# Lower halves of four w_up blocks made on GpSimd in a hybrid decoder layer

## Chip, cores and metric

The kernel runs on one core of one Trainium2 chip. The metric is the device time of one execution in microseconds; of several executions the median is given. The engines are called TensorE (PE in the rows; its weight loads are PEld), VectorE (DVE), ScalarE (ACT), GpSimd (POOL) and SyncE (SP, which issues most DMAs here).

## What is computed

One decoder layer on a sequence of 512 tokens with 1024 features, all in float32. An attention group and a recurrent group share one input projection; their outputs are joined by w_out, normalised and added to x; then comes a gated feed-forward part with a causal convolution of width 3 and another norm. Cut to what matters here:

```python
    mix = jnp.concatenate([attn, lru], axis=-1) @ w_out[l].astype(h.dtype)
    x = x + rms_norm(mix, g_post_mix[l])
    h = rms_norm(x, g_pre_ffn[l])
    up = causal_dwconv(h @ w_up[l].astype(h.dtype), w_conv_ffn[l], b_conv_ffn[l])
    c_u, c_g = jnp.split(up, 2, axis=-1)
    ffn = (jax.nn.gelu(c_g, approximate=True) * c_u) @ w_down[l].astype(h.dtype)
    x = x + rms_norm(ffn, g_post_ffn[l])
```

w_up is 1024 x 5632: 22 blocks of 128 columns for c_u and 22 for c_g.

## The kernel before

Every large product is made of three TensorE products on halves: a float32 operand is split into an upper half h (a rounded copy in the type that TensorE reads, made by ScalarE) and a lower half l = x - h, made by VectorE unless `split` is given another engine (L83 to L85). `mm3` (L77 to L81) then issues h times h (L79), one h with the other's l (L80) and the reverse (L81). `split_w` (L92) does it for a piece of a weight, 128 x 1024 here, from a tile `raw` that a DMA filled; there are four buffers for each half and two for `raw`.

The place in question is the passage from w_out to w_up. `wide` (L738) makes the product with w_out in two column halves; in the second one, for the token tiles t = 0 to 3 of 128 rows each, 24 products go into `py`t (L79 to L81), then `weighted` (L713) squares the result on ScalarE, multiplies it by the gain on VectorE (L725) and makes the reciprocal root `rpost` (L135 to L141: small 128x1 operations), and `mixed` (L768) adds it to the residual `xres` (two operations at L733), squares that on ScalarE (`sqn`, L150), makes `rpre` in the same way, scales (`hn`, L154), transposes on TensorE (`ptr`, L160, eight in two banks), and splits the result into h2Th (ScalarE, L84) and h2Tl (VectorE, L85, reading the bank). So tile after tile goes through a chain over VectorE, ScalarE and TensorE.

Meanwhile the first four blocks of w_up have been split into tiles of their own (`fw00` to `fw11`, `load_first_up`, L787). The loop at L833 takes four blocks a turn, `i2` = 0 to 10: two of c_u and two of c_g. For i2 = 0 the products run in two column halves of 256 tokens (L842 to L844), so that the first half needs only the tiles t = 0 and 1; that makes 96 products of 256 columns for each half. For i2 = 1 and on, four `split_w` calls (L839) make the blocks, and the products have 512 columns. For i2 = 1 these splits have no other work ahead of them than the chain of the norm.

Up to L182 the order of instructions on each engine is the written one. Behind it a scheduler orders them by its own estimate, engine by engine, as buffers and data come free; each engine then works its list strictly in order. In the list of VectorE the four subtractions of i2 = 1 (tiles wl_2498, wl_2503, wl_2508 and wl_2513) stand between the steps of the chain.

Of the kernel before, what the change touches and what calls it, by code (L numbers as in the profile page):

```python
# [18 lines left out]
P = 128  # L19
# [8 lines left out]
KD = D // P  # L28
# [24 lines left out]
def hybrid_layer(  # L53
# [6 lines left out]
    nc = tc.nc  # L60
# [9 lines left out]
    def bank(name, tag):  # L70
        return ps.tile([P, 512], F32, tag=tag, name=name, bufs=BANKS[tag])
# [11 lines left out]
    def split(h, l, src, sub=None):  # L83
        nc.scalar.copy(h, src)  # L84
        (sub or nc.vector).tensor_sub(l, src, f32(h))  # L85

    def load_raw(src, k, n):
        t = wp.tile([P, k, n], F32, tag="raw", name="raw", bufs=2)
        nc.sync.dma_start(t, src.rearrange("(k p) n -> p k n", p=P))
        return t  # L90

    def split_w(src, k, n, sub=None):  # L92
        h = wp.tile([P, k, n], F32R, tag="wh", name="wh")
        l = wp.tile([P, k, n], F32R, tag="wl", name="wl")
        split(h, l, src, sub)
        return h, l
# [688 lines left out]
    first_up = [[], []]  # L785
# [26 lines left out]
    def up(w, pt, c0, c1):  # L812
        for k in range(KD):
            mm3(pt[:, c0:c1], at(w, slice(None), k), at(h2T, slice(None), k, slice(c0, c1)),
                k == 0, k == KD - 1)
# [9 lines left out]
    def glu(i, pu, pg):  # L825
        yu = conv(pu, i, "yu")
        yg = conv(pg, NF + i, "yg")
        nc.scalar.activation(yg, yg, AF.Gelu_apprx_tanh)  # L828
        nc.vector.tensor_mul(yu, yu, yg)  # L829
        split(*act_at(i, slice(None)), yu)  # L830

    up_tags = itertools.cycle(("mm", "sc", "mm", "sc", "mm", "av"))
    for i2 in range(NF // 2):  # L833
        if i2:
            raws = [load_raw(w_up[:, o + 256 * i2:o + 256 * (i2 + 1)], KD, 256) for o in (0, DFF)]
        blocks = [[], []]
        for b in range(2):
            for j in range(2):
                w = split_w(raws[j][:, :, b * P:(b + 1) * P], KD, P) if i2 else first_up[b][j]  # L839
                blocks[b].append((w, bank("pup", next(up_tags))))  # L840
        if i2 == 0:
            for c0, c1 in ((0, S // 2), (S // 2, S)):  # L842
                for w, pt in blocks[0] + blocks[1]:
                    up(w, pt, c0, c1)  # L844
        for b in range(2):
            if i2:
                for w, pt in blocks[b]:
                    up(w, pt, 0, S)
            glu(2 * i2 + b, blocks[b][0][1], blocks[b][1][1])
        if i2 == 0:  # L850
            f_stack.close()
            actp2 = ctx.enter_context(tc.tile_pool(name="actp2", bufs=1, side="right"))
            acts.append([actp2.tile([P, NF - NF1, S], F32R, name=f"act{i}") for i in "hl"])
# [45 lines left out]
```

## Time and profile before

| | us |
|---|---|
| median of 3 runs | 585.64 (584.77 to 586.01) |
| the profiled execution | 584.45 |
| its span, first to last instruction | 582.3 |
| TensorE busy | 571.0 (98%) |
| VectorE busy | 360.1 (62%) |
| ScalarE busy | 279.3 (48%) |
| GpSimd busy | 15.9 (3%), the last of it at 96 us |

A row of a timeline gives the start, the duration, the engine, the line, the operation and what it writes and reads; in brackets, how long the engine was idle ahead of it and what ended that. Successive instructions of one engine overlap a little in their rows, so the step from start to start is shorter than a duration.

### The profile page before, as it was taken

The numbers are of one execution on the slowest core, as the hardware profiler recorded it, in microseconds if no ns is written. First come the engines' busy times: TensorE is split into PE (matmuls) and PEld (weight loads), VectorE is DVE, ScalarE is ACT, GpSimd is POOL, SyncE is SP. The second block draws the span as 40 slices with busy tenths as digits, with TensorE's granted clock in tenths as the row PEclk, the third lists the DMA queues.
The fourth block names the chain that finished last, engine by engine and source line by source line (L and its number), as shares of the span: only waits on it lengthen the run. The fifth ranks groups of instructions, "written<-read, shape, count | busy, mean of one in ns | idle before, by whom it ended". The sixth has DMA issues, their size and how long they took to land.

```text
span 582.3 us, 7051 instructions
## 1 busy us (share of the span) xinstructions
PE 571.0 (98%) x2734; PEld 472.9 (81%) x2734; DVE 360.1 (62%) x649; ACT 279.3 (48%) x457; POOL 15.9 (3%) x37
## 2 busy tenths in 40 slices
PE   8999999999999999999999999999999999999995
PEld 4988887887788789888888888888888888888884
DVE  5797777889896895656656656656656521241225
ACT  6568846868776663543443444444444321132121
POOL 2150000000000000000000000000000000000000
PEclk9999999999999999999999999999999999999998
DMA  9533627333202614013412412412413222332103
GB/s 275 152 110 122 205 72 200 94 106 108 74 1 72 217 41 142 1 49 96 145 55 90 144 60 86 146 64 81 144 66 136 88 72 90 100 136 73 37 0 144
DMA packets 53450, 59.62 MB, mean 102 GB/s; under 512 B 2481, under 2 KB 42625, under 8 KB 53418
## 3 DMA queue, kind: packets, MB, share of 16 engines
q1 hardware_dynamic: 53319, 59.11, 31.9%
q8 instruction: 21, 0.34, 0.2%
q14 instruction: 12, 0.09, 0.1%
q10 hardware_dynamic: 98, 0.07, 0.0%
HBM read 57.06 MB, written 3.69 MB: 104 GB/s over the span
## 4 chain that ended last, share of the span: by engine, by line
PE 90%; DVE 4%; ACT 3%; DMA 2%; issue 0%; DVEq 0%; SPq 0%; ACTq 0%
PE pup L80 14%; PE pup L81 14%; PE pup L79 14%; PE py L80 8%; PE py L79 8%; PE py L81 8%; PE px L309 3%; PE pq L79 2%; PE pq L80 2%; PE pq L81 2%; PE pav L663 2%; PE ptp L653 1%; PE pgr L81 1%; PE pgr L80 1%; PE pv L81 1%; PE pv L80 1%
## 5 line engine op out<-in xcount | busy, mean ns | idle before, releaser
L85 DVE TENSOR_TENSOR wl<-raw,wh 128x1024 fp32r<-128x1024 f32 x78 | 95.3, 1222 | 125.4 <-ACT wh L84 125.1
L84 ACT CAST wh<-raw 128x1024 fp32r<-128x1024 f32 x78 | 81.7, 1049 | 139.7 <-PE py L81 71.7
L80 PE MATMUL pup<-h2Tl,wh 128*128 128x512 f32 x320 | 124.5, 389 | 0.0
L81 PE MATMUL pup<-h2Th,wl 128*128 128x512 f32 x320 | 124.5, 389 | 0.0
L79 PE MATMUL pup<-h2Th,wh 128*128 128x512 f32 x320 | 124.3, 389 | 0.0
L80 PEld LDWEIGHTS pup<-h2Tl,wh 128*128 128x128 f32 x320 | 60.1, 188 | 12.5
L79 PEld LDWEIGHTS pup<-h2Th,wh 128*128 128x128 f32 x320 | 60.0, 188 | 12.5
L81 PEld LDWEIGHTS pup<-h2Th,wl 128*128 128x128 f32 x320 | 60.1, 188 | 12.3
L79 PE MATMUL py<-wh,acth 128*128 128x512 f32 x176 | 68.5, 389 | 0.0
L80 PE MATMUL py<-wl,acth 128*128 128x512 f32 x176 | 68.5, 389 | 0.0
L81 PE MATMUL py<-wh,actl 128*128 128x512 f32 x176 | 68.5, 389 | 0.0
L79 PEld LDWEIGHTS py<-wh,acth 128*128 128x128 f32 x176 | 33.0, 188 | 6.9
L81 PEld LDWEIGHTS py<-wh,actl 128*128 128x128 f32 x176 | 33.0, 188 | 6.9
L80 PEld LDWEIGHTS py<-wl,acth 128*128 128x128 f32 x176 | 33.0, 188 | 6.7
L821 DVE SCALAR_TENSOR_TENSOR yu<-pup,par,yu 128x511 f32<-128x511 f32 (+1 forms) x44 | 32.9, 749 | 4.3 <-ACT yu L819 3.5
L828 ACT ACTIVATE yg<-yg 128x512 f32<-128x512 f32 x22 | 13.9, 632 | 44.6 <-DVE yg L821 44.6
L821 DVE SCALAR_TENSOR_TENSOR yg<-pup,par,yg 128x511 f32<-128x511 f32 (+1 forms) x44 | 32.8, 746 | 2.0 <-ACT yg L819 1.2
L829 DVE TENSOR_TENSOR yu<-yu,yg 128x512 f32<-128x512 f32 x22 | 15.2, 693 | 18.0 <-ACT yg L828 18.0
L81 PE MATMUL py<-wh,mixTl 128*128 128x512 f32 x64 | 25.4, 397 | 0.0
L79 PE MATMUL pq<-hTh,wh 128*128 128x512 f32 x64 | 25.4, 397 | 0.0
L81 PE MATMUL pq<-hTh,wl 128*128 128x512 f32 x64 | 25.3, 395 | 0.0
L79 PE MATMUL py<-wh,mixTh 128*128 128x512 f32 x64 | 25.2, 394 | 0.0
(213 smaller groups left out, 938.2 us busy)
## 6 DMA issues: line engine op xcount, KB each, us to landing
raw<-in_w_up_dram SPq DMA_DIRECT2D x22, 1024.0 KB, 5.1
raw<-in_w_down_dram SPq DMA_DIRECT2D x10, 1024.0 KB, 5.3
raw<-in_w_in_dram SPq DMA_DIRECT2D x4, 1024.0 KB, 5.2
rawqk<-in_w_in_dram SPq DMA_DIRECT2D x8, 512.0 KB, 5.3
raw<-in_w_out_dram SPq DMA_DIRECT2D x4, 1024.0 KB, 5.6
raw<-in_w_in_dram SPq DMA_DIRECT2D x4, 512.0 KB, 9.1
out_dram<-yz SPq DMA_DIRECT2D x8, 256.0 KB, 2.0
xres<-in_x_dram SPq DMA_DIRECT2D x3, 512.0 KB, 5.8
```

Source lines behind the costliest of these rows:

```text
L79: nc.tensor.matmul(o, lh, rh, start=start, stop=False)
L80: nc.tensor.matmul(o, lh, rl, start=False, stop=False)
L81: nc.tensor.matmul(o, ll, rh, start=False, stop=stop)
L84: nc.scalar.copy(h, src)
L85: (sub or nc.vector).tensor_sub(l, src, f32(h))
L309: nc.tensor.matmul(p_x[t][:, cs], w_x[t][i == LH][:, k], hT[i == HL][:, k, cs], start=first and n == 0, stop=last and n == len(todo) - 1)
L653: nc.tensor.transpose(ptr[:, j * P:(j + 1) * P], st[:, j * P:(j + 1) * P], ident)
L663: nc.tensor.matmul(pav[:, j * P:], vs, pT[i][:, j * S:j * (S - P) + S], start=j == 0 and i == 0, stop=j == NT - 1 and i == 1)
L821: nc.vector.scalar_tensor_tensor(y[:, d:], pt[:, :S - d], w_conv_f(2 - d, blk), y[:, d:], op0=ALU.mult, op1=ALU.add)
L828: nc.scalar.activation(yg, yg, AF.Gelu_apprx_tanh)
L829: nc.vector.tensor_mul(yu, yu, yg)
```

## The change

For i2 = 1 the lower halves of the four blocks are subtracted by GpSimd; for i2 = 2 and on by VectorE as before.

```diff
-                w = split_w(raws[j][:, :, b * P:(b + 1) * P], KD, P) if i2 else first_up[b][j]
+                w = first_up[b][j] if i2 == 0 else split_w(
+                    raws[j][:, :, b * P:(b + 1) * P], KD, P, nc.gpsimd if i2 == 1 else None)
```

What GpSimd has behind its last operation of before, the clearing of klz (the tile names with a number are single tiles, `raw_2493` and `raw_2495` the two loaded pieces):

```order
L596 MEMSET klz_897 64x512
L85 TENSOR_TENSOR wl_2498<-raw_2493,wh_2497 128x1024 [waits DVE_49,DMAHW6_49,Activation_49,Pool_49]
L85 TENSOR_TENSOR wl_2503<-raw_2495,wh_2502 128x1024 [waits DMAHW7_49,DVE_49,Activation_49]
L85 TENSOR_TENSOR wl_2508<-raw_2493,wh_2507 128x1024 [waits DVE_49,Activation_49]
L85 TENSOR_TENSOR wl_2513<-raw_2495,wh_2512 128x1024 [waits DVE_49,PE_49,Activation_49]
```

Before, only the first row and the program's end stand there.

The scheduler then orders the neighbours anew. On VectorE, from the end of tile 1's small operations (rpre_2114) to its h2Tl (from ptr_2121), there stood before:

```order
L141 SCALAR_TENSOR_TENSOR rpre_2114<-rpre_2114 128x1 [waits DVE_49]
L141 SCALAR_TENSOR_TENSOR rpost_2161<-rpost_2161 128x1 [waits DVE_49]
L85 TENSOR_TENSOR wl_2498<-raw_2493,wh_2497 128x1024 [waits DMAHW6_49,Activation_49]
L154 SCALAR_TENSOR_TENSOR hn_2110<-xres_66,rpre_2114,gpre_ffn_1812 128x1024 [waits DVE_49]
L733 SCALAR_TENSOR_TENSOR xres_66<-yg2_1818,rpost_2161,xres_66 128x512 [waits DVE_49]
L733 SCALAR_TENSOR_TENSOR xres_66<-yg2_1818,rpost_2161,xres_66 128x512
L725 TENSOR_TENSOR yg3_1819<-py3_1974,gpost_mix_1810 128x512 [waits Activation_49]
L85 TENSOR_TENSOR h2Tl_1815<-ptr_2121,h2Th_1814 128x4x128 [waits Activation_49]
L85 TENSOR_TENSOR h2Tl_1815<-ptr_2128,h2Th_1814 128x4x128 [waits Activation_49]
```

And now, in the same place on VectorE:

```order
L141 SCALAR_TENSOR_TENSOR rpre_2114<-rpre_2114 128x1 [waits DVE_49]
L141 SCALAR_TENSOR_TENSOR rpost_2161<-rpost_2161 128x1 [waits DVE_49]
L154 SCALAR_TENSOR_TENSOR hn_2110<-xres_66,rpre_2114,gpre_ffn_1812 128x1024 [waits DVE_49]
L733 SCALAR_TENSOR_TENSOR xres_66<-yg2_1818,rpost_2161,xres_66 128x512 [waits DVE_49]
L733 SCALAR_TENSOR_TENSOR xres_66<-yg2_1818,rpost_2161,xres_66 128x512
L85 TENSOR_TENSOR h2Tl_1815<-ptr_2121,h2Th_1814 128x4x128 [waits Activation_49]
L85 TENSOR_TENSOR h2Tl_1815<-ptr_2128,h2Th_1814 128x4x128 [waits Activation_49]
```

The subtraction of wl_2498 is gone ahead of hn_2110, and L725 for tile 3 has moved behind the h2Tl of tile 1; the other three subtractions of before stood further on, ahead of tile 2's hn and residual sums.

On TensorE, the last products with w_out for tile 3 (py3), tile 1's transposes and the first up-products, before:

```order
L80 MATMUL py3_1974<-wl_1992,mixTh_94 128x512
L81 MATMUL py3_1974<-wh_1991,mixTl_95 128x512
L160 MATMUL ptr_2121<-ident_77,hn_2110 128x128 [waits DVE_49,PE_49]
L160 MATMUL ptr_2121<-ident_77,hn_2110 128x128 x3
L160 MATMUL ptr_2128<-ident_77,hn_2110 128x128 [waits PE_49]
L160 MATMUL ptr_2128<-ident_77,hn_2110 128x128 x3
L79 MATMUL pup_2267<-h2Th_1814,fw00h_1999 128x256 [waits Activation_49]
L79 MATMUL pup_2268<-h2Th_1814,fw01h_2003 128x256
L79 MATMUL pup_2269<-h2Th_1814,fw10h_2007 128x256
L79 MATMUL pup_2270<-h2Th_1814,fw11h_2011 128x256
L80 MATMUL pup_2267<-h2Tl_1815,fw00h_1999 128x256 [waits DVE_49]
```

And now, in the same place on TensorE:

```order
L160 MATMUL ptr_2121<-ident_77,hn_2110 128x128 [waits DVE_49,PE_49]
L160 MATMUL ptr_2121<-ident_77,hn_2110 128x128 x3
L160 MATMUL ptr_2128<-ident_77,hn_2110 128x128 [waits PE_49]
L160 MATMUL ptr_2128<-ident_77,hn_2110 128x128 x3
L80 MATMUL py3_1974<-wl_1992,mixTh_94 128x512
L81 MATMUL py3_1974<-wh_1991,mixTl_95 128x512
L79 MATMUL py3_1974<-wh_1991,mixTh_94 128x512
L80 MATMUL py3_1974<-wl_1992,mixTh_94 128x512
L81 MATMUL py3_1974<-wh_1991,mixTl_95 128x512
L79 MATMUL pup_2267<-h2Th_1814,fw00h_1999 128x256 [waits Activation_49]
L80 MATMUL pup_2267<-h2Tl_1815,fw00h_1999 128x256 [waits DVE_49]
```

Tile 1's transposes have moved ahead of the last five of py3's 24 products, and of the up-products only one, not four, stands ahead of the first that needs h2Tl. Further on, tile 2's transposes stand behind 35 up-products (before: 45) and tile 3's behind 68 (before: all 96 of the first half), and the two 512-column products with wh that stood early among the second half's are back in their own place. On ScalarE the cast of wh_2512 stands a little later, behind tile 2's roots; on SP's queue the load of raw_2637 (i2 = 2) stands ahead of that of gpost_ffn, and this load and that of raw_2639 wait for GpSimd.

## Rows read from the trace of the kernel before

**Rows 1.** Stretches: length, busy of PE, PEld, DVE, ACT, POOL, granted clock, DMA share, GB/s

```profile
210.00:230.00 20.00, 19.00 (x149) 17.71 (x148) 15.17 (x29) 8.28 (x17) 0.00 (x0) 1.00 0.41 132
460.00:520.00 60.00, 60.00 (x267) 49.67 (x266) 18.03 (x25) 15.23 (x21) 0.00 (x0) 1.00 0.29 96
```

**Rows 2.** Timeline of TensorE, 205 to 239 us

```profile
205.22 0.39 PE L79 MATMUL py<-wh,mixTh 128*128 128x512 f32 x1
...
210.44 0.39 PE L81 MATMUL py<-wh,mixTl 128*128 128x512 f32 x1
210.96 1.06 PE L160 MATMUL ptr<-ident,hn 128*128 128x128 f32 x8
212.27 0.39 PE L79 MATMUL pup<-h2Th,fw00h 128*128 128x256 f32 x1 [0.24 <-ACT h2Th L84]
...
213.40 0.39 PE L80 MATMUL pup<-h2Tl,fw00h 128*128 128x256 f32 x1 [0.39 <-DVE h2Tl L85]
213.62 0.28 PE L81 MATMUL pup<-h2Th,fw00l 128*128 128x256 f32 x1
...
218.41 1.04 PE L160 MATMUL ptr<-ident,hn 128*128 128x128 f32 x8
219.20 0.36 PE L80 MATMUL pup<-h2Tl,fw01h 128*128 128x256 f32 x1
...
225.47 1.06 PE L160 MATMUL ptr<-ident,hn 128*128 128x128 f32 x8
226.77 0.39 PE L79 MATMUL pup<-h2Th,fw00h 128*128 128x256 f32 x1 [0.24 <-ACT h2Th L84]
...
238.84 0.40 PE L80 MATMUL pup<-h2Tl,wh 128*128 128x512 f32 x1
```

**Rows 3.** Timeline of ScalarE, around 16 us and 205 to 222 us

```profile
16.23 1.04 ACT L297 CAST wh<-raw 128x1024 fp32r<-128x1024 f32 x1
...
205.24 1.07 ACT L150 ACTIVATE sqn<-xres 128x1024 bf16<-128x1024 f32 x1
...
207.23 2.00 ACT L84 CAST wh<-raw 128x1024 fp32r<-128x1024 f32 x2
...
211.63 1.08 ACT L84 CAST h2Th<-ptr 128x512 fp32r<-128x512 f32 x2
...
221.88 1.06 ACT L150 ACTIVATE sqn<-xres 128x1024 bf16<-128x1024 f32 x1 [1.76 <-DVE xres L733]
```

**Rows 4.** Timeline of VectorE, 208 to 225 us

```profile
208.40 1.23 DVE L85 TENSOR_TENSOR wl<-raw,wh 128x1024 fp32r<-128x1024 f32 x1
209.54 1.28 DVE L154 SCALAR_TENSOR_TENSOR hn<-xres,rpre,gpre_ffn 128x1024 f32<-128x1024 f32 x1
210.73 1.41 DVE L733 SCALAR_TENSOR_TENSOR xres<-yg,rpost,xres 128x512 f32<-128x512 f32 x2
...
224.03 1.29 DVE L154 SCALAR_TENSOR_TENSOR hn<-xres,rpre,gpre_ffn 128x1024 f32<-128x1024 f32 x1
```

**Rows 5.** Timelines of GpSimd and VectorE, 10 to 20 us; L139 (min/median/max ns)

```profile
10.55 2.38 POOL L300 TENSOR_TENSOR wl<-raw,wh 128x1024 fp32r<-128x1024 f32 x1 [8.27 <-ACT wh L297]
10.91 0.68 DVE L291 TENSOR_TENSOR hTl<-ptr,hTh 128x512 fp32r<-128x512 f32 x1
...
17.35 2.39 POOL L300 TENSOR_TENSOR wl<-raw,wh 128x1024 fp32r<-128x1024 f32 x1 [4.41 <-ACT wh L297]
17.49 2.26 DVE L139 SCALAR_TENSOR_TENSOR rpre<-rpre 128x1 f32<-128x1 f32 x1
...
L139 DVE SCALAR_TENSOR_TENSOR rpre<-rpre x8: 220/220/2258, 6.4 to 223.6; 128x1 f32<-128x1 f32 x8
```

**Rows 6.** Timelines of VectorE and GpSimd, 31 to 33 us

```profile
31.59 1.23 DVE L510 TENSOR_TENSOR gwl<-graw,gwh 128x1024 fp32r<-128x1024 f32 x1
31.71 1.16 POOL L495 TENSOR_TENSOR sp<-sp 128x4 f32<-128x4 f32 x1 [2.68 <-DVE sp L494]
```

**Rows 7.** A stretch at the kernel's end, columns as in rows 1

```profile
578.00:580.00 2.00, 0.00 (x0) 0.00 (x0) 1.39 (x2) 0.00 (x0) 0.00 (x0) 0.53 0.19 76
```

## The prediction

> **What bounds the kernel now.** I read the stretches first. From 460 to 520 us TensorE is busy 60.00 of 60.00, and so it is in every stretch from 230 us to the last products. The stretch from 210 to 230 us has 19.00 of 20.00 [rows 1]. So every microsecond that TensorE loses or wins before 230 us goes straight into the span, and this is where the four lower halves are made. The next view is TensorE's own order of time there [rows 2]. Four 128-row tiles (t = 0 to 3) are normalised, transposed on TensorE (L160) and split into h2Th (ScalarE) and h2Tl (VectorE), while TensorE fills in with products. At tile 1 it runs dry: the transposes start at 210.96, the first up-product at 212.27, the first that needs h2Tl at 213.40. At tile 3 the transposes at 225.47 are followed by a product only at 226.77. In between products follow each other at 0.12 us ((225.47 - 219.20) / 51 steps of 256 columns) or 0.227 us ((210.44 - 205.22) / 23 steps of 512). What TensorE waits for is the chain of the norm on VectorE and ScalarE, so those two are read last [rows 3, 4].
>
> **What is removed, and what that is worth alone.** Four VectorE subtractions of 128x1024 leave the chain. The one at 208.40 stands straight ahead of tile 1's hn, which starts at 209.54 [rows 4]. Without it hn starts at 208.40 and ends 1.28 later, at 209.68. The scheduler also puts tile 1's transposes after 19 of py3's 24 products instead of behind all 24. TensorE reaches that place at 205.22 + 19 x 0.227 = 209.53 and waits till 209.82 (hn's end + 0.14, as 210.96 follows 209.54 + 1.28). Transposes take 0.79 (218.41 to 219.20), the five products left 1.13 and 0.1 for the restart: the first up-product goes at 211.84. ScalarE's cast starts 0.67 after the transposes (211.63 against 210.96 [rows 2, 3]), so 210.49 to 211.08 for the first half, and the first half of h2Tl ends near 211.8: the product that needs it, at 211.96, does not wait. Before, four up-products were done at 213.40; after, they would be done at 211.84 + 0.1 + 4 x 0.12 = 212.4. With the restart at 213.40 (0.22 to the next, not 0.12) the lead is 1.1 us. At tile 3, 1.30 us go by from 225.47 to 226.77; after, the transposes stand among products, with 0.79, a restart of 0.1 and a wait of some 0.3 for hn, another 0.15 less. Sum without any side effect: **-1.25 us**.
>
> What moves elsewhere costs nothing. The loads of the third w_up pair wait for GpSimd instead of VectorE, and gpost_ffn's load now stands behind the first of them on SP's queue; the third pair is used after the 96 products of 0.227 us of the second, 22 us later than that one, and gpost_ffn in the last stage. The four lower halves themselves are needed only after the 192 first up-products, from 238.84 on.
>
> **What is added: four GpSimd subtractions on a path shared with VectorE.** The same operation stands in the trace twice, at 10.55 and 17.35, with 2.38 and 2.39 us [rows 5]. Beside the second, VectorE's 128x1 operation of L139, 0.22 at the median of its eight, starts at 17.49 and takes 2.26: it ends at 19.75, GpSimd at 19.74. It reads two operands from SBUF. The other way round, VectorE's two-operand subtraction runs 31.59 to 32.82, and GpSimd's 128x4 operation started at 31.71 takes 1.16, to 32.87 [rows 6]. The hTl subtraction at 10.91 has one operand in PSUM and keeps its 0.68 beside GpSimd. So two SBUF operands on VectorE and a GpSimd operation exclude each other, and whoever came first keeps the path till its end.
>
> No row shows two long ones in turn. The Trainium skill, "SBUF — State Buffer", section "Who interferes with whom", says that a VectorE instruction with two SBUF inputs contends with a GpSimd one that reads SBUF, and that whoever issues first has the port pair for the whole instruction. The rows agree (2.26 against 0.22). By this rule the change costs what is worked out next; if only tiny operations suffered, it would be the -1.25 above.
>
> On VectorE in this stretch L139, L141, hn (L154) and both residual sums (L733) read two SBUF operands; h2Tl and L725 have one in PSUM. Now the walk, with GpSimd and VectorE taking turns:
>
> The first GpSimd operation is released by the first of the two casts that start at 207.23 (1.05 us; 0.08 on, as 17.35 follows 16.23 + 1.04 [rows 3, 5]): 208.36. hn of tile 1 asks at 208.40. Whoever wins, the other waits.
>
> *VectorE first.* hn to 209.68, GpSimd one to 212.06, first residual sum to 212.75, GpSimd two to 215.13, second sum to 215.8. Only then, by program order, comes tile 1's h2Tl, its first half ready at 216.5. TensorE stands there since 211.96: **4.5 us lost**. GpSimd three runs beside h2Tl. ScalarE's squares of tile 2 need the second sum, so they start at 215.8; from there hn follows after 3.16 (205.24 to 208.40 [rows 3, 4]) at 218.97, and the fourth GpSimd operation after 1.99 + 1.05 + 0.08 at 218.92. If GpSimd wins again, tile 2's hn ends at 222.5 and TensorE, which has done its 34 products at 220.7, waits 1.9 more; if hn wins, the residual sums of tile 3 come late instead (two in 1.41 [rows 4], after GpSimd's 222.6), tile 3's squares start at 224.0 and its hn 2.15 later (221.88 to 224.03), and TensorE waits about as long at tile 3. Both ways the 192 products end near 243.5, where before they ended at 238.84 - 2 x 0.227 = 238.39: **+5.1 us**.
>
> *GpSimd first.* It holds till 210.74, hn ends at 211.95, tile 1's transposes start at 212.1 instead of 209.5: 2.55 us lost. Then GpSimd two to 214.3, sum to 215.0, GpSimd three to 217.4, sum to 218.1, h2Tl's first half at 218.75. TensorE came there at 214.25: 4.5 us lost again. Tile 2 and the fourth operation meet as before, some 2 us. The 192 products end near 246: **+7.6 us**.
>
> The two differ by 0.04 us in who asks first, which no row decides. I take the middle, **+6.3 us**. The profiled execution took 584.45 us for a span of 582.3; the median of the runs is 585.64. A shift before 230 us moves both alike: 590.8 for the profile's own, and 585.64 + 6.3 = 591.9, rounded to 592.0, for the median.
>
> One thing is on top and has no row of its size. From 578 to 580, at the kernel's end, TensorE has nothing left to do and its granted clock is 0.53 on average, so it is at the lower of its two levels, 1.2 GHz, for most of that [rows 7]; in the stretches of [rows 1] it is 1.00. A stall of 4.5 us in the middle could let it fall too. Lower bound 0; upper bound, if it stays at half speed as long as the stall was, 4.5 / 2 = 2.2 us. Since the trace shows no such fall at work I take 0 for the forecast and keep 2.2 for the range.
>
> **The rivals.**
> 1. *VectorE keeps the path while it has work in a row* (for: its next operation starts 0.07 before the last one's end; against: the other engine has been waiting). Then the sums follow hn directly and GpSimd gets in only where VectorE waits or works from PSUM. With hn first at 208.40: GpSimd one at 210.93, two at 213.4 to 215.8, which holds tile 2's L139 and so its hn (1.4 us of stall); three and four meet tile 3's. 192 products end at 238.6 to 240.9: +0.2 to +2.5. With GpSimd first at 208.36: 2.5 us at tile 1, 1.4 at tile 2, the rest: 240.9, +2.5. Time 585.8 to 588.1.
> 2. *Long operations pass each other* after all, and the chain gets its 1.14 us: -1.25, 584.4, faster. For: a 128x1024 subtraction that waits is nowhere in the trace. Against: [rows 5, 6], both directions.
> 3. *The clock falls in the stall*: +7 to +9.8, 592.6 to 595.4.
>
> **How the numbers follow.** Taking turns, the clock staying up: 0.50, at 590.5 to 593.5. Clock falls: 0.12. VectorE keeps the path: 0.27, of which 0.09 lies so near to +0.2 us that it is within 0.2% (1.2 us, about what a measurement of this kernel can tell from no change). No conflict: 0.11, of which 0.08 is a gain over 1.2 us or a little more with luck, 0.03 within. So faster 0.08, same 0.12, slower 0.80. The range reaches from the lower end of rival 1, 585.8, to 595.0: it leaves out rival 2 and the upper end of rival 3.
>
> **What would show it.** Right: GpSimd's four operations at 208 to 222 with durations or starts that interlock with hn and L733; one VectorE 128x1 or 128x512 operation of 2 us or more; a TensorE wait of about 4.5 us for h2Tl (L85) ahead of the first L80 product, and waits of about 2 us for hn ahead of transposes; everything after 250 us shifted as a block, TensorE busy again all the time. The prediction is wrong if VectorE's hn and sums keep 1.28 and 0.75 beside running GpSimd operations (rival 2), if the sums follow hn without a gap while GpSimd's operations stretch to 4 us (rival 1), or if the granted clock leaves 1.00 after the stall (rival 3).

## The result and the profile after

The changed kernel took 591.35 us (median, 590.36 to 592.24) beside 585.32 for the kernel before: ratio 1.0106, 95% interval 1.0091 to 1.012, slower by 6.0 us where 6.3 had been forecast. Timed once more on another chip (below) it took 592.36 beside 584.94, ratio 1.0131 (1.0117 to 1.0145), slower by 7.4. The profiled execution took 590.36 us, with a span of 588.1 (584.45 and 582.3 before).

Stretches of the changed kernel, columns as in [rows 1]:

```profile
210.00:230.00 20.00, 16.39 (x104) 15.40 (x105) 17.63 (x25) 7.59 (x16) 8.21 (x3) 0.83 0.40 132
460.00:520.00 60.00, 60.00 (x266) 49.70 (x265) 17.23 (x22) 14.81 (x18) 0.00 (x0) 1.00 0.29 97
```

TensorE is busy for 16.39 of the 20 us in which it was busy for 19.00 [rows 1], at a granted clock of 0.83 on average where it was 1.00; from 460 us on it is full, as before. So the loss lies where the prediction put it, and goes through to the end whole: the last product starts at 581.21, before at 575.47, 5.74 later; the first product of i2 = 1 starts at 244.13, before at 238.84 - 2 x 0.227 = 238.39 [rows 2], 5.74 later too. Tile 0's transposes and the last product before, then these two and the first product of i2 = 1 in the changed kernel:

```profile
203.59 1.09 PE L160 MATMUL ptr<-ident,hn 128*128 128x128 f32 x8 [0.21 <-DVE hn L154]
...
575.47 0.39 PE L81 MATMUL py<-wh,actl 128*128 128x512 f32 x1
```

```profile
202.56 1.09 PE L160 MATMUL ptr<-ident,hn 128*128 128x128 f32 x8 [0.17 <-DVE hn L154]
...
244.13 0.40 PE L79 MATMUL pup<-h2Th,wh 128*128 128x512 f32 x1
...
581.21 0.39 PE L81 MATMUL py<-wh,actl 128*128 128x512 f32 x1
```

Who held the path is read from GpSimd and VectorE side by side. GpSimd's four subtractions in the changed kernel, and under them VectorE (the row with x2 covers both residual sums, the one above it the first of them alone):

```profile
207.38 2.38 POOL L85 TENSOR_TENSOR wl<-raw,wh 128x1024 fp32r<-128x1024 f32 x1 [112.71 <-DVE rpre L141]
...
209.71 3.34 POOL L85 TENSOR_TENSOR wl<-raw,wh 128x1024 fp32r<-128x1024 f32 x1
...
213.02 2.81 POOL L85 TENSOR_TENSOR wl<-raw,wh 128x1024 fp32r<-128x1024 f32 x1
219.52 2.39 POOL L85 TENSOR_TENSOR wl<-raw,wh 128x1024 fp32r<-128x1024 f32 x1 [3.69 <-ACT wh L84]
```

```profile
207.36 3.49 DVE L154 SCALAR_TENSOR_TENSOR hn<-xres,rpre,gpre_ffn 128x1024 f32<-128x1024 f32 x1
...
210.77 2.84 DVE L733 SCALAR_TENSOR_TENSOR xres<-yg,rpost,xres 128x512 f32<-128x512 f32 x1
...
210.77 5.61 DVE L733 SCALAR_TENSOR_TENSOR xres<-yg,rpost,xres 128x512 f32<-128x512 f32 x2
216.30 1.27 DVE L85 TENSOR_TENSOR h2Tl<-ptr,h2Th 128x512 fp32r<-128x512 f32 x2
...
219.55 3.44 DVE L154 SCALAR_TENSOR_TENSOR hn<-xres,rpre,gpre_ffn 128x1024 f32<-128x1024 f32 x1
222.91 1.40 DVE L733 SCALAR_TENSOR_TENSOR xres<-yg,rpost,xres 128x512 f32<-128x512 f32 x2
...
226.93 1.28 DVE L154 SCALAR_TENSOR_TENSOR hn<-xres,rpre,gpre_ffn 128x1024 f32<-128x1024 f32 x1
```

A recorded duration here includes the time in which an operation stands started and waits. Read the ends. GpSimd's first subtraction takes its plain 2.38 and ends at 209.76; hn, 1.28 in [rows 4], is stretched to 3.49 and ends at 210.85, 1.09 later. GpSimd's second has been standing since 209.71; it ends at 213.05, 2.20 behind hn. The first residual sum ends at 213.61, 0.56 behind that, GpSimd's third at 215.83, the second sum at 216.38: GpSimd, VectorE, GpSimd, VectorE, GpSimd, VectorE without an exception. h2Tl, with one operand in PSUM, takes its 1.27 for the two, but GpSimd is idle then; it stands beside a subtraction in "VectorE first" below. At tile 2 the same: GpSimd 219.52 to 221.91, hn to 222.99. Tile 3 meets nobody and keeps 1.28.

What TensorE makes of it, in its own timeline:

```profile
210.99 1.94 PE L160 MATMUL ptr<-ident,hn 128*128 128x128 f32 x8 [2.33 <-DVE hn L154]
...
217.03 0.39 PE L80 MATMUL pup<-h2Tl,fw00h 128*128 128x256 f32 x1 [2.12 <-DVE h2Tl L85]
...
218.11 0.41 PE L81 MATMUL pup<-h2Th,fw00l 128*128 128x256 f32 x1
218.32 0.41 PE L79 MATMUL pup<-h2Th,fw00h 128*128 128x256 f32 x1
...
223.13 1.07 PE L160 MATMUL ptr<-ident,hn 128*128 128x128 f32 x8 [0.29 <-DVE hn L154]
```

It waits 2.33 us for tile 1's hn and 2.12 for h2Tl. After the first wait the transposes take 1.94 and not 1.06, and at 218 us products of 256 columns follow each other at 0.21 us and not 0.12. The stretches say why: TensorE is busy throughout both, at the lower clock level.

```profile
211.00:214.00 3.00, 3.00 (x11) 2.72 (x12) 3.00 (x2) 1.17 (x2) 3.00 (x2) 0.50 0.00 0
218.00:221.00 3.00, 3.00 (x16) 3.00 (x16) 2.83 (x9) 1.44 (x5) 1.48 (x1) 0.50 1.10 382
```

### The profile page after: what moved, and what is told of

It reads as the page before. It is cut to its first block, busy times and chain, and to the rows that moved or that the text cites. A ratio compares the mean times of both kernels' runs of the same rounds, so it can differ in the third digit from the quotient of the medians.

```text
span 588.1 us, 7055 instructions
## 1 busy us (share of the span) xinstructions
PE 573.5 (98%) x2734; PEld 475.3 (81%) x2734; DVE 364.6 (62%) x645; ACT 279.1 (47%) x457; POOL 26.8 (5%) x41
## 4 chain that ended last, share of the span: by engine, by line
PE 89%; DVE 5%; ACT 4%; DMA 1%; issue 0%; DVEq 0%; ACTq 0%
PE pup L80 13%; PE pup L81 13%; PE pup L79 13%; PE py L81 8%; PE py L79 8%; PE py L80 8%; PE px L309 3%; PE pq L79 2%; PE pq L80 2%; PE pq L81 2%; PE pav L663 2%; DVE hn L154 2%; PE ptp L653 1%; PE pgr L81 1%; PE pv L81 1%; PE pv L80 1%
## 5 line engine op out<-in xcount | busy, mean ns | idle before, releaser
L85 DVE TENSOR_TENSOR wl<-raw,wh 128x1024 fp32r<-128x1024 f32 x74 | 90.5, 1222 | 126.0 <-ACT wh L84 125.8
L80 PE MATMUL pup<-h2Tl,wh 128*128 128x512 f32 x320 | 124.6, 389 | 0.0
L80 PEld LDWEIGHTS pup<-h2Tl,wh 128*128 128x128 f32 x320 | 60.1, 188 | 12.3
L80 PE MATMUL py<-wl,acth 128*128 128x512 f32 x176 | 68.5, 389 | 0.0
L80 PEld LDWEIGHTS py<-wl,acth 128*128 128x128 f32 x176 | 33.0, 188 | 6.8
L80 PE MATMUL py<-wl,mixTh 128*128 128x512 f32 x64 | 25.8, 403 | 0.0
```

Of the source, the lines that this page charges most:

```text
L80: nc.tensor.matmul(o, lh, rl, start=False, stop=False)
```

## The experiments

To compare kernels without the variation of the stages ahead (tile 0's transposes start anywhere from 202.56 to 204.62 us in these profiles), the passage is measured from tile 0's transposes to the first product of i2 = 1, behind the 192 up-products. Where two of that block's products stand early, as before, they are put back at 0.227 each. Before: 238.39 - 203.59 = 34.80 us.

| kernel | passage, us | against before | median beside before | ratio (95%) |
|---|---|---|---|---|
| changed | 41.57 | +6.77 | 591.35 / 585.32 | 1.0106 (1.0091 to 1.012) |
| changed, again | 42.24 | +7.44 | 592.36 / 584.94 | 1.0131 (1.0117 to 1.0145) |
| GpSimd only writes | 33.45 | -1.35 | 583.87 / 584.75 | 0.9986 (0.9977 to 0.9995) |
| GpSimd late | 33.45 | -1.35 | 584.0 / 584.75 | 0.9983 (0.9974 to 0.9992) |
| VectorE late | 33.45 | -1.35 | 583.18 / 584.75 | 0.9974 (0.9965 to 0.9983) |
| extra reads behind the chain | 34.79 | -0.01 | 584.71 / 584.75 | 1.001 (0.9991 to 1.003) |
| extra reads in the chain | 40.87 | +6.07 | 590.72 / 584.91 | 1.010 (1.0085 to 1.0115) |
| only the last block | 36.42 | +1.62 | 586.45 / 584.91 | 1.0017 (1.0001 to 1.0034) |
| GpSimd copies | 34.82 | +0.02 | 585.12 / 584.91 | 1.0003 (0.9994 to 1.0013) |
| VectorE first | 39.38 | +4.58 | 589.75 / 584.94 | 1.0082 (1.0068 to 1.0095) |

The ratio is not that of the two medians: it comes from all the executions, so a single long one counts in it (590.68 among those of the extra reads behind the chain).

### GpSimd only writes

The order of every other engine is that of the changed kernel; GpSimd is at work in the chain of tile 1 too, but reads nothing. The kernel leaves the four lower halves out: they are zeros.

```diff
-        (sub or nc.vector).tensor_sub(l, src, f32(h))
+        if sub is nc.gpsimd:
+            for _ in range(2):
+                sub.memset(f32(l), 0.0)
+        else:
+            nc.vector.tensor_sub(l, src, f32(h))
```

> On the four blocks GpSimd clears the lower halves twice each instead of subtracting (8 clears of 128x1024, some 0.96 us each as the clearing of graw takes in the trace of before), so the lower halves are zeros and GpSimd writes SBUF but reads nothing. Every other engine has the order of the changed kernel. Theory (VectorE's operations with two SBUF operands and GpSimd's SBUF reads exclude each other): hn and the residual sums keep 1.28 and 1.41 a pair, no long wait of TensorE, and the new order gives its 1.25 us: about 584.1. Rival (the new order by itself costs the time): stays near 591.4. Rival (any GpSimd access excludes VectorE, writes too): the clears interlock with hn and the sums, some +2 to +6 us, 587 to 591.

Measured: 583.87, faster than before. GpSimd's timeline, then VectorE's (L158 is hn, L737 the sums):

```profile
206.92 7.47 POOL L87 MEMSET wl<- 128x1024 f32 x8 [110.94 <-PE py L80]
```

```profile
208.68 1.28 DVE L158 SCALAR_TENSOR_TENSOR hn<-xres,rpre,gpre_ffn 128x1024 f32<-128x1024 f32 x1
209.87 1.41 DVE L737 SCALAR_TENSOR_TENSOR xres<-yg,rpost,xres 128x512 f32<-128x512 f32 x2
```

Eight writes run without a pause from 206.92 to 214.39, and hn and both sums in their midst keep 1.28 and 1.41. So neither the new order of instructions nor a busy GpSimd costs anything. What is left is that a subtraction reads SBUF and is longer (2.38 against 0.93); the copies further on separate these two. This is also the kernel in which the freed 1.14 us is seen alone: the passage is 1.35 us shorter.

### The subtractions behind the chain, on either engine

Each lower half first gets one element copied from tile 3's h2Tl, so that it is made after the chain: by GpSimd in one kernel, by VectorE in the other.

```diff
+        if sub is nc.gpsimd:
+            sub.tensor_copy(l[:, 0, 0:1], f32(late[0][:, KD - 1, S - 1:S]))
         (sub or nc.vector).tensor_sub(l, src, f32(h))
...
+    late.append(h2T[1])
```

In the second kernel a line `sub = nc.vector` stands ahead of the copy.

> The changed kernel, but GpSimd first copies one element of tile 3's last h2Tl into each of the four lower-half tiles, so that its four subtractions come after the whole chain of the norm and no earlier. The order on TensorE, VectorE and ScalarE is that of the changed kernel. Theory (the loss is GpSimd's subtractions meeting the chain): no meeting, the chain gets its 1.25 us, the subtractions run from about 228 to 238 us and are ready when TensorE needs them one after the other from 237 us on: 584.1, faster than both kernels. Rival (order costs): 591. Rival (GpSimd comes too late and TensorE waits for it): a TensorE wait for the first of the four at 237 us, 585 or more.

> As the run with the late GpSimd subtractions, but VectorE makes all four, after tile 3's h2Tl; GpSimd does nothing. Theory: what helps is that the subtractions leave the chain, whoever makes them: also 584.1, with VectorE busy with them for 4 x 1.15 = 4.6 us from about 228 us and the first gated blocks' convolution some 1.3 us later, which TensorE does not feel. Rival (the gain of the late run needs GpSimd): 585.3, as before.

Measured: 584.0 and 583.18, both faster than before, with the same passage of 33.45. GpSimd's timeline of the first, and VectorE's of the second:

```profile
225.04 9.50 POOL L89 TENSOR_TENSOR wl<-raw,wh 128x1024 fp32r<-128x1024 f32 x4
```

```profile
224.86 3.50 DVE L90 TENSOR_TENSOR wl<-raw,wh 128x1024 fp32r<-128x1024 f32 x3
...
228.46 1.23 DVE L90 TENSOR_TENSOR wl<-raw,wh 128x1024 fp32r<-128x1024 f32 x1
```

Four GpSimd subtractions end at 234.54, VectorE's at 229.69, both ahead of the first product of their blocks (237.61 and 237.84). The work costs nothing there, on whichever engine. The second kernel beats both the kernel before and the changed one (why it is 0.8 us ahead of the first, with the same passage, no run tells): what the four operations needed was another time, not another engine.

### The same reads added to the kernel before

The lower halves stay on VectorE and in their old places; GpSimd makes a subtraction of the same kind into a spare tile that nobody reads. In the first form the tile lay in a pool that comes free late; in the second it lies in another one and is 128x768.

```diff
+    spare = edge.tile([P, 6, P], BF16, name="spare")
...
+                if i2 == 1:
+                    nc.gpsimd.tensor_sub(spare, raws[j][:, 0:6, b * P:(b + 1) * P], f32(w[0][:, 0:6]))
```

> The kernel before with all its orders, VectorE still makes all lower halves, and GpSimd makes the same four subtractions a second time into a spare tile that nobody reads. Theory (exclusion): the loss comes although nothing that is used has moved and no order has changed; VectorE's own four subtractions now take part in the turns too, so more than in the changed kernel, +6 to +10 us: 591 to 595. Rival (the new order, or the new waits on GpSimd, cost the time): 585.3.

> As the run with the extra GpSimd subtractions, but into a spare tile that is free early, so that they start as soon as the upper halves are there (208 us); three quarters of a block each (128x768), about 1.8 us. All orders are those of the kernel before, and VectorE makes the four lower halves that are used. Theory (exclusion, taking turns): GpSimd's operations interlock with VectorE's wl, hn and residual sums; hn of tile 1 ends some 3.5 us later, h2Tl of tile 1 about 5 us; +5 to +7 us, 590 to 592. Rival (the loss came from the new order or the new waits on GpSimd): 584.8.

The first form missed its aim, since GpSimd waited for the tile until 226.72 and worked behind the chain: 584.71, no change. It stands as a control. The second was in the chain: 590.72, slower by 5.8. GpSimd, VectorE and TensorE of the second form:

```profile
208.35 7.86 POOL L842 TENSOR_TENSOR spare<-raw,wh 128x768 bf16<-128x768 f32 x3 [112.67 <-DVE rpre L141]
```

```profile
208.32 1.23 DVE L85 TENSOR_TENSOR wl<-raw,wh 128x1024 fp32r<-128x1024 f32 x1
209.46 2.86 DVE L154 SCALAR_TENSOR_TENSOR hn<-xres,rpre,gpre_ffn 128x1024 f32<-128x1024 f32 x1
212.25 4.51 DVE L733 SCALAR_TENSOR_TENSOR xres<-yg,rpost,xres 128x512 f32<-128x512 f32 x2
```

```profile
218.01 0.38 PE L80 MATMUL pup<-h2Tl,fw00h 128*128 128x256 f32 x1 [3.50 <-DVE h2Tl L85]
...
244.83 0.40 PE L80 MATMUL pup<-h2Tl,wh 128*128 128x512 f32 x1
```

No instruction of another engine has moved and nobody waits for the spare tile; the added subtractions alone give the loss. With the order of before, this kernel also prices the clock. From the first product that needs h2Tl to that block's first L80 product it takes 244.83 - 218.01 = 26.82 us, before 238.84 - 213.40 = 25.44 [rows 2], and TensorE waits for nothing new in between. The granted clock is 0.50 from 220 to 222, and 0.67 and 0.62 in the microseconds around: the 1.38 us are the price of the clock.

```profile
220.00:222.00 2.00, 2.00 (x11) 2.00 (x11) 2.00 (x3) 0.00 (x0) 1.50 (x1) 0.50 0.07 27
```

### Only the last block on GpSimd

```diff
-                    raws[j][:, :, b * P:(b + 1) * P], KD, P, nc.gpsimd if i2 == 1 else None)
+                    raws[j][:, :, b * P:(b + 1) * P], KD, P, nc.gpsimd if i2 == 1 and b and j else None)
```

> Only the fourth of the four lower halves (wl_2513) is made by GpSimd; the order is near that of the kernel before, with VectorE making the other three in the chain. Theory (exclusion): GpSimd's one operation asks at about 214.8, in the middle of VectorE's wl_2503, runs from 215.1 to 217.5 and holds up L139, wl_2508 and hn of tile 2, which ends about 2 us later; TensorE waits some 1.8 us for tile 2's transposes and less for tile 3's: +1.3 us, 585.5 to 586.8. Rival (a lower half taken off VectorE is a gain whenever the order stays): -0.3 to -0.6 us, 584.3.

Measured: 586.45, slower by 1.5 in the median; the ratio's interval only just excludes no change, the passage is 1.62 longer. GpSimd, VectorE, TensorE:

```profile
215.45 2.63 POOL L85 TENSOR_TENSOR wl<-raw,wh 128x1024 fp32r<-128x1024 f32 x1 [119.16 <-ACT wh L84]
```

```profile
215.74 0.15 DVE L138 RECIPROCAL rpre<-rpre 128x1 f32<-128x1 f32 x1
...
215.93 2.17 DVE L139 SCALAR_TENSOR_TENSOR rpre<-rpre 128x1 f32<-128x1 f32 x1
...
219.42 1.27 DVE L154 SCALAR_TENSOR_TENSOR hn<-xres,rpre,gpre_ffn 128x1024 f32<-128x1024 f32 x1
```

```profile
220.83 1.06 PE L160 MATMUL ptr<-ident,hn 128*128 128x128 f32 x8 [1.64 <-DVE rpost L141]
```

One meeting is enough. The reciprocal, with one operand in SBUF, keeps 0.15 while the subtraction already stands started; the 128x1 operation of L139 with two takes 2.17 and ends with GpSimd, at 218.10 and 218.08. TensorE's transposes of tile 2 wait 1.64 us for the hn behind it (the row names the small operation that ended last; hn ends at 220.69, 0.14 ahead of the transposes).

### GpSimd copies

In place of the subtraction GpSimd copies `raw` into the lower half: one operand in SBUF, not two. The kernel leaves out the subtraction, so its lower halves are not those of the layer. The order is that of the changed kernel.

```diff
-        (sub or nc.vector).tensor_sub(l, src, f32(h))
+        if sub is nc.gpsimd:
+            sub.tensor_copy(l, src)
+        else:
+            nc.vector.tensor_sub(l, src, f32(h))
```

> The changed kernel with all its orders, but GpSimd copies the raw block into the four lower halves instead of subtracting, so it reads one operand, and the lower halves are wrong by the upper ones. Theory (any SBUF read of GpSimd excludes VectorE's operations with two SBUF operands): the copies, 1 to 2 us each, take turns with hn and the sums like the subtractions, with less to wait for: +1 to +5 us, 586 to 590. Rival (only a two-operand GpSimd operation needs the shared path): as with the clears, about 583.9.

Measured: 585.12, below the 586 to 590 that had been expected, and 1.25 above the kernel that only writes (its passage 1.37 longer). The size was missed; the rows decide between theory and rival. GpSimd, then VectorE (L142 is the former L139):

```profile
208.98 1.05 POOL L86 CAST wl<-raw 128x1024 fp32r<-128x1024 f32 x1 [0.26 <-DVE rpost L141]
210.34 2.12 POOL L86 CAST wl<-raw 128x1024 fp32r<-128x1024 f32 x1 [0.31 <-PE py L80]
```

```profile
208.96 1.07 DVE L142 SCALAR_TENSOR_TENSOR rpre<-rpre 128x1 f32<-128x1 f32 x1
...
210.27 1.28 DVE L157 SCALAR_TENSOR_TENSOR hn<-xres,rpre,gpre_ffn 128x1024 f32<-128x1024 f32 x1
211.47 2.19 DVE L736 SCALAR_TENSOR_TENSOR xres<-yg,rpost,xres 128x512 f32<-128x512 f32 x2
```

A copy excludes VectorE just as well: L142 ends with the copy at 210.03, the next copy waits for hn (2.12 and not 1.05), the first sum for that copy. It costs less because a copy holds the path for 1.05 us, not for 2.38, and because only two of the four copies meet an operation with two SBUF operands: the first, at 207.68, and the last, at 213.75, beside h2Tl, meet none. The Trainium skill, "SBUF — State Buffer", section "Who interferes with whom", draws the line between a GpSimd instruction that reads SBUF and one that only writes it; the 1.07 beside a copy and the 1.28 beside the writes agree.

### VectorE first

GpSimd clears its first tile (twice and a quarter) ahead of its first subtraction, so that this asks a little after hn. The changed kernel ran once more beside it.

```diff
+        if sub is nc.gpsimd and not begun:
+            for d in (KD, KD, 2):
+                sub.memset(f32(l[:, 0:d]), 0.0)
+            begun.append(l)
         (sub or nc.vector).tensor_sub(l, src, f32(h))
```

> GpSimd first clears the tile of its first lower half (twice and a quarter), so that its first subtraction asks a few tenths of a us after tile 1's hn instead of a few hundredths before it; all other orders are those of the changed kernel. Theory (whoever issues first holds the path, then strict turns): hn of tile 1 keeps 1.28, GpSimd's first subtraction waits for hn's end, the first residual sum waits for it (some 2.8), the second for the next; the second sum ends one turn of GpSimd (about 2.1 us) sooner than in the changed kernel and the whole chain with it: about 589 (588.3 to 589.8), TensorE's wait for tile 1's hn gone. Rival (four meetings cost the same in whatever order): 591, the wait only moves from hn to h2Tl.

> The changed kernel once more, on the chip of the run beside it: 591 (590.3 to 592.3), hn of tile 1 with about 3.5, TensorE's waits 2.3 for hn and 2.1 for h2Tl.

Measured: 589.75 and 592.36, on the same chip; the second lies just above its expected range. GpSimd's first three subtractions, VectorE with hn first, then TensorE:

```profile
210.00 8.37 POOL L91 TENSOR_TENSOR wl<-raw,wh 128x1024 fp32r<-128x1024 f32 x3
```

```profile
209.33 1.28 DVE L160 SCALAR_TENSOR_TENSOR hn<-xres,rpre,gpre_ffn 128x1024 f32<-128x1024 f32 x1
210.53 5.62 DVE L739 SCALAR_TENSOR_TENSOR xres<-yg,rpost,xres 128x512 f32<-128x512 f32 x2
216.07 1.27 DVE L91 TENSOR_TENSOR h2Tl<-ptr,h2Th 128x512 fp32r<-128x512 f32 x2
...
219.32 3.44 DVE L160 SCALAR_TENSOR_TENSOR hn<-xres,rpre,gpre_ffn 128x1024 f32<-128x1024 f32 x1
```

```profile
216.80 0.58 PE L80 MATMUL pup<-h2Tl,fw00h 128*128 128x256 f32 x1 [3.71 <-DVE h2Tl L91]
...
222.91 1.07 PE L166 MATMUL ptr<-ident,hn 128*128 128x128 f32 x8 [0.44 <-DVE hn L160]
```

hn keeps 1.28, the wait for it is gone, and from hn's start to the end of the second sum it takes 216.15 - 209.33 = 6.82 us, in the changed kernel 216.38 - 207.36 = 9.02. One turn of GpSimd less is worth 2.6 us in the median. The rival, that the wait would only move, falls. This kernel also shows h2Tl, with its one operand in PSUM, beside a subtraction: GpSimd's third ends at 218.37, and both h2Tl, from 216.07 on, keep 1.27.

The changed kernel again, TensorE and one stretch of it:

```profile
212.66 1.06 PE L160 MATMUL ptr<-ident,hn 128*128 128x128 f32 x8 [2.33 <-DVE hn L154]
...
218.71 0.58 PE L80 MATMUL pup<-h2Tl,fw00h 128*128 128x256 f32 x1 [3.71 <-DVE h2Tl L85]
...
225.49 1.03 PE L160 MATMUL ptr<-ident,hn 128*128 128x128 f32 x8
```

```profile
218.00:224.00 6.00, 5.29 (x24) 5.29 (x25) 5.62 (x13) 3.03 (x7) 2.37 (x1) 0.50 0.81 262
```

The meetings are the same as in the first profile (hn 3.49, sums 5.61, and hn 3.42 at tile 2), the clock is not. After the same 2.33 us without work it stayed up here, so TensorE came to h2Tl earlier and waited 3.71, not the 2.12 of the first profile that had been expected again. Behind that wait it ran at half clock for 6 us. Tile 2's hn ended at 224.64 (221.22 + 3.42, as recorded), and the transposes could have gone some 0.14 later; they went at 225.49, without a wait. So 0.7 us was lost to the clock here, which is the 0.67 by which the two passages of one kernel differ.

## Why the prediction was right, and where it was not

**What bounds the kernel, and that a loss passes through whole**: right; 5.74 us at 244 us and 5.74 at the last product.

**What the removal is worth** (-1.25): right. The three kernels that have the new order without a read of GpSimd's in the chain show -1.35 in the passage, and -0.75 to -1.6 by medians. That loads, queues and the late use of the lower halves cost nothing is shown by the same three.

**That a two-operand operation of VectorE and a GpSimd operation that reads exclude each other, in turns**: right, the step on which all hung. Rival 1 (VectorE keeps the path) falls with the first sum: it was ready behind hn and still let GpSimd's second pass, 2.84 against some 0.7. Rival 2 (long ones pass) falls with hn's 3.49.

**The middle of two walks** (+6.3 between +5.1 and +7.6): the number was right, the step was not a case that occurs. GpSimd came first in both profiles, and the walk for that case is the one to compare: +7.6 forecast, +6.77 and +7.44 in the passage. The other walk's case was made by force: +5.1 forecast, +4.58 in the passage, +4.8 by medians. The first timing gave +6.0 and the second +7.4. So it is luck that 6.3 lies within 0.3 of the first timing: the walk for the case that occurred was 0.8 too long in the passage, and tile 0's transposes stood 1.03 us earlier than before. In the profiles the difference between the two timings is, besides 0.67 in the passage, in the stage ahead: tile 0's transposes started at 202.56 in the first and at 204.22 in the second, before at 203.59. Why, no run tells.

**The terms of the walk with GpSimd first.** 2.55 us lost at tile 1's transposes: 2.33 as a wait. 4.5 us for h2Tl: mis-sized by 0.8; it is 3.71 where the clock had stayed up. A waiting operation that is let in needs less than its duration, since part of that had gone by while it waited: hn 1.09 and not 1.28, a sum 0.55 and not 0.7, GpSimd 2.2 and not 2.38. In the recorded sum hn's end (211.95) is reckoned with 1.21 us, in the other walk with 1.28, which is too little to matter. Some 2 us at tile 2: about right, by rows alone. TensorE would have been at tile 2's transposes 34 x 0.12 us after the first product that needs h2Tl, at 222.8 in the second profile, and hn came at 224.64.

**Clock, taken as 0 with 2.2 in the range**: the fall did happen, in both profiles, so as a statement on the mechanism "the clock staying up" was wrong and rival 3 had too small a chance. Its price was about what was taken: nothing in the first profile, by its rows, because both half-clock stretches ended in a wait for VectorE's chain, which set the time anyway (2.12 us and 0.29 us were still left to wait); 0.7 us in the second; 1.38 us where TensorE had work of its own behind the stall. That the first profile lost nothing was argued from its waits and not tried by itself.

**The signs named in advance**: interlocked hn and sums, a 128x512 sum of over 2 us (2.84), some 2 us of waiting for tile 1's hn (2.33) and the shift as a block came. The wait for h2Tl came, but as 2.12 and 3.71 and not 4.5. A stretched 128x1 operation came only in other kernels (2.17 with only the last block, 1.07 beside a copy). One of the signs of being wrong came as well: the granted clock left 1.00 (rival 3).

## What to carry to other kernels

Before moving work to an idle GpSimd, look at what VectorE does at that time: if its operations there read two operands from SBUF and stand in a chain that others wait for, every GpSimd operation that reads SBUF can put its whole length into the chain, and one is enough. If the work isn't needed yet, move it in time instead: behind the chain it was free on either engine, and that gave the gain which the change was to bring. In a kernel that TensorE bounds, a stall of some microseconds costs itself and then up to another 1.4 us of half clock, unless the next wait swallows that.

## What had not been expected of the hardware

- The clock fell after waits of 2.3 to 3.7 us, in the changed kernel to 0.50 for about 3 us in two places or for 6 in one, and not the same way each time: the same 2.33 us without work, in the same program, was followed by half clock in one run and by full clock in the other.
- Who comes first can't be read from recorded starts that lie 0.03 us apart. hn stood started at 207.36 and GpSimd at 207.38, and GpSimd had the path; with 208.32 and 208.35 (extra reads in the chain) VectorE had it. With 210.27 against 210.34 and 209.33 against 210.00 it was VectorE.
- GpSimd's copy of 128x1024 takes 1.05 us, its subtraction 2.38 and its clearing 0.93 (7.47 for eight). The copy blocks as the subtraction does, the clearing not at all.
